# The seams around the feed-forward of a hybrid layer: four output tiles by token halves, plain products placed between the second norm's matmuls, other places and queues where down begins

## The chip, the core and the metric

One core of a Trainium2 chip runs the whole kernel as one program. Its engines run beside each other, each through its own list of instructions: TensorE (PE: matmuls, and loads of their weights), VectorE (DVE), ScalarE (ACT), GpSimd (POOL) and SyncE (SP, which here only issues transfers). An instruction waits until what it reads is there and what it overwrites has been read; all that stands behind it on the same engine waits with it. The metric is the time of one execution on the device in microseconds (us), the median of several runs.

## The reference

One layer, cut to what matters here: the matmuls around the second norm and the shapes. The two mixers ahead of it are not touched.

```python
D_MODEL = 1024; SEQ = 1024; D_FF = 2816; EPS = 1e-6     # BATCH 1, DEPTH 1, all float32

def rms_norm(x, w):
    y = x * lax.rsqrt(jnp.mean(x * x, axis=-1, keepdims=True) + EPS)
    return y * w

def reference(x, norm1_w, w_in, ..., w_out, norm2_w, w_gate, w_up, w_down):
    h = rms_norm(x, norm1_w[l])
    z, xbc, dt_raw, q, k, v = jnp.split(h @ w_in[l], SPLITS, axis=-1)
    y_ssd = ssd_mixer(z, xbc, dt_raw, ...)          # causal convolution, chunked state scan, gated norm
    y_att = diff_attention(q, k, v, ...)            # 8 heads, difference of two softmax maps, head norm
    x = x + jnp.concatenate([y_ssd, y_att], axis=-1) @ w_out[l]         # (1024, 2048) @ (2048, 1024)
    h = rms_norm(x, norm2_w[l])
    return x + (jax.nn.silu(h @ w_gate[l]) * (h @ w_up[l])) @ w_down[l] # 2816 wide in between
```

## The kernel before

Channels lie on the 128 partitions and the 1024 tokens along the free axis, so the model's width is 8 tiles (DK), and a matmul makes 128 channels by 512 tokens, one "token half" (`halves`). float32 products are made of three matmuls: each operand is split into a high part (a cast by ScalarE, line 152) and a low part (operand minus high part, line 153, by VectorE or GpSimd), and `mm3` (lines 163 to 166) adds high x high, high x low and low x high. A piece of weights is loaded by SP into a `wr` buffer, of which there are two, and split (`load_op`).

The **out projection** has eight output tiles. `add_out(d, q...)` puts one quarter of the inner width for tile d on a list of jobs, and `half()` works jobs off. Tiles 0 to 5 take both token halves with one load of each weight piece; tiles 6 and 7 are done for the first half of the tokens, then for the second, with their weights loaded once for each half: 6 x 4 + 2 x 4 x 2 = 40 pieces of 256 KB. After each tile `out_post` (line 1031) adds the residual into `x2[d]`, stores it to `x2d` in DRAM (SP), and sums its squares into `accm`. When a token half is complete, a job `norm2(hf)` follows (line 1045): four matmuls that sum `accm` over the channels (`ps_r2`, line 1050), mean and power -1/2, a transpose (`ps_tr`, line 117), its spreading over a row (line 123), a matmul that broadcasts that row to all partitions (`ps_bc`, line 135), its copy into `accm` by ScalarE (line 136), eight scalings of `x2[d]` by VectorE (line 1059), and eight splits into the operands `a11`, `a12` (first half of the tokens) or `a21`, `a22` (second half).

The **feed-forward** has 22 tiles of 128 inner channels. Two of them are done by plain products (`plain`, line 1108): 24 matmuls, three for each of the 8 tiles of channels, for one tile, for gate or up (u = 0 or 1) and one token half. The first three, (f, u, hf) = (0, 0, 0), (0, 1, 0) and (1, 0, 0), need only the first half's operands; the rest needs the second's. In between GpSimd makes sums and differences of the operands (`sums`, lines 1077 to 1083) for the other 20 tiles, which follow Strassen's scheme with seven products over 2 x 2 blocks instead of eight. The first of these products is `ps_a`.

Gate times up gives `m`. `store_pair` (line 1087) stores for each pair of tiles seven operands of down's seven products into `md` in DRAM: three stores of `m`, and four of sums that GpSimd makes (`ss`, `sd`, lines 1096 to 1104). **Down** takes the 11 pairs in four chunks (3, 3, 3, 2 pairs) and the 8 output tiles in four pairs: a *unit* is a chunk and a pair of output tiles, 7 products of 9 matmuls (6 in the last chunk). `fetch_m` (line 1259) brings the stored operands back into `mr` buffers (four, issued by GpSimd) and splits them into `mo`; `Down.load` brings a unit's weights (`wr`, `in_wdn_dram`, 768 KB, issued by SP); GpSimd makes differences of them (`t`, line 1151) and `make` (line 1288) casts and subtracts. In the first chunk `fetch_m` for all seven products stands ahead of the units; for the other chunks it stands behind each product of the chunk's last unit (`Ahead`). The sums go to `acc` tiles that are loaded from `x2d` (line 1325, eight of 512 KB, GpSimd). Down's tiles lie where those of gate/up lay, since the pools of the latter are closed first; a write there waits for the last reader of what lay there.

The order of instructions on each engine is not the order of the code: a list scheduler with modelled durations picks, when the program is built, the next ready instruction of each engine. What the code fixes is what depends on what, the pools, and the queue on which a transfer is issued.

## Time and profile before

| | |
|---|---|
| median of 3 runs | 1706.17 us (1706.12 to 1708.75) |
| the profiled execution | 1707.36 us |
| its span, first to last instruction | 1705.6 us, 23840 instructions |
| PE busy | 1630.9 us, 96 %, 8237 matmuls |
| VectorE, GpSimd, ScalarE busy | 68 %, 46 %, 46 % |
| DRAM read and written | 107.99 MB, 34.87 MB |

The profile is of one execution. Its span and the 1.8 us around it make the execution's time. "Busy" counts time in which the engine has an instruction under way; a timeline lists an engine's instructions by start, with the idle time before each in brackets and what ended it. SPq in place of SP is that engine's issuing of transfers.

### The profile page before, as it was taken

The page shows a single profiled execution, that of the slowest core. Times are in us where ns is not written, and L with a number is a line of the kernel's source. Part 1 is how long each engine was busy: PE and PEld are TensorE (multiplying, and loading weights), DVE is VectorE, ACT ScalarE, POOL GpSimd, SP SyncE. Part 2 cuts the span into 40 slices and gives each one's busy share as a digit, 9 for nine tenths or more (in the row PEclk, how much of TensorE's full clock was granted, in tenths as well). Part 3 has the DMA queues.
Part 4 walks back from the last instruction along what each step waited for, and adds up shares of the span by engine and source line. Part 5 has one row for each costly group of instructions (what it writes and reads, how often), then busy time and mean ns, then how long its engine had stood idle before and what let it go on. Part 6 is the DMA issues. An engine that isn't in the chain of part 4 may idle for free.

```text
span 1705.6 us, 23840 instructions
## 1 busy us (share of the span) xinstructions
PE 1630.9 (96%) x8237; PEld 1383.0 (81%) x8237; DVE 1155.7 (68%) x2213; ACT 782.3 (46%) x1751; POOL 786.4 (46%) x988
## 2 busy tenths in 40 slices
PE   7899999999999999999999987999999999499998
PEld 7799999999988787877778866888888888388886
DVE  7788788878887567886641249855555554498876
ACT  5576676666565544546321234332333222354531
POOL 5755665665522323333242219644344441565535
PEclk9899999999999999999999988999999999699999
DMA  5100110110011110132152312322332221655533
GB/s 185 38 26 26 50 44 15 43 50 14 14 62 44 50 38 27 49 142 81 62 179 74 106 43 68 136 99 99 105 102 102 99 93 44 253 183 162 162 104 111
DMA packets 72312, 144.40 MB, mean 85 GB/s; under 512 B 8362, under 2 KB 16810, under 8 KB 72192
## 3 DMA queue, kind: packets, MB, share of 16 engines
q1 hardware_dynamic: 53984, 108.93, 18.8%
q0 software_dynamic: 8704, 29.24, 5.2%
q10 hardware_dynamic: 9504, 4.72, 1.0%
q8 instruction: 65, 1.06, 0.3%
q14 instruction: 55, 0.45, 0.1%
HBM read 107.99 MB, written 34.87 MB: 84 GB/s over the span
## 4 chain that ended last, share of the span: by engine, by line
PE 86%; DVE 6%; issue 3%; ACT 2%; DMA 1%; POOL 1%; DVEq 0%; ACTq 0%; POOLq 0%
PE ps_pj L203 5%; PE ps_pj L205 5%; PE ps_pj L204 5%; PE ps_x L481 5%; PE ps_x L482 4%; PE ps_x L483 4%; PE p L166 4%; PE p L165 4%; PE p L164 3%; PE ps_c L164 3%; PE ps_a L166 3%; PE ps_c L165 3%; PE ps_d L166 3%; PE ps_c L166 3%; PE ps_d L164 3%; PE ps_d L165 3%
## 5 line engine op out<-in xcount | busy, mean ns | idle before, releaser
L152 ACT CAST op<-wr 128x512 fp32r<-128x512 f32 x148 | 91.2, 618 | 260.4 <-PE p L166 94.9
L153 DVE TENSOR_TENSOR op<-wr,op 128x512 fp32r<-128x512 f32 x104 | 85.6, 825 | 151.5 <-ACT op L152 143.6
L203 PE MATMUL ps_pj<-wh,xwh 128*128 128x384 f32 (+1 forms) x512 | 175.6, 346 | 6.8 <-ACT wh L146 6.0
L205 PE MATMUL ps_pj<-wh,xwl 128*128 128x384 f32 (+1 forms) x512 | 173.7, 341 | 3.5 <-DVE xwl L270 3.5
L204 PE MATMUL ps_pj<-wl,xwh 128*128 128x384 f32 (+1 forms) x512 | 174.0, 340 | 0.0
L1151 POOL TENSOR_TENSOR t<-wr,t 128x512 f32<-128x512 f32 (+2 forms) x72 | 92.5, 1285 | 152.8 <-issue 123.7
L153 POOL TENSOR_TENSOR op<-wr,op 128x512 fp32r<-128x512 f32 x44 | 58.8, 1336 | 224.8 <-ACT op L152 224.8
L481 PE MATMUL ps_x<-xwh,op 128*128 128x512 f32 x320 | 129.8, 406 | 0.9 <-ACT ya L424 0.9
L482 PE MATMUL ps_x<-xwl,op 128*128 128x512 f32 x320 | 126.7, 396 | 0.0
L483 PE MATMUL ps_x<-xwh,op 128*128 128x512 f32 x320 | 126.5, 395 | 0.0
L1151 POOL TENSOR_TENSOR t<-wr 128x512 f32<-128x512 f32 (+2 forms) x72 | 87.9, 1221 | 62.9 <-DVE op L153 32.9
L378 ACT ACTIVATE pt<-ps_s,nm 128x640 f32<-128x640 f32 (+7 forms) x128 | 94.3, 740 | 44.5 <-DVE nm L373 24.3
L203 PEld LDWEIGHTS ps_pj<-wh,xwh 128*128 128x128 f32 x512 | 97.5, 191 | 7.4 <-ACT wh L146 7.1
L166 PE MATMUL p<-y,op 128*128 128x512 f32 x256 | 101.3, 398 | 0.0
L165 PE MATMUL p<-y,op 128*128 128x512 f32 x256 | 101.2, 397 | 0.0
L205 PEld LDWEIGHTS ps_pj<-wh,xwl 128*128 128x128 f32 x512 | 97.4, 190 | 4.2 <-DVE xwl L270 4.2
L152 ACT CAST op<-t 128x512 fp32r<-128x512 f32 x80 | 49.6, 622 | 111.4 <-PE ps_c L166 53.9
L164 PE MATMUL p<-y,op 128*128 128x512 f32 x256 | 99.5, 399 | 0.0
L153 DVE TENSOR_TENSOR op<-t,op 128x512 fp32r<-128x512 f32 x80 | 77.2, 967 | 31.9 <-ACT op L152 30.9
L204 PEld LDWEIGHTS ps_pj<-wl,xwh 128*128 128x128 f32 x512 | 97.7, 191 | 0.4
L373 DVE TENSOR_REDUCE nm<-ps_s 128x1 f32<-128x640 f32 (+7 forms) x128 | 93.7, 745 | 1.4
L318 POOL TENSOR_TENSOR raw<-raw,w_qk 128x192 f32<-128x192 f32 x56 | 41.1, 734 | 79.4 <-ACT raw L317 46.3
(302 smaller groups left out, 4754.6 us busy)
## 6 DMA issues: line engine op xcount, KB each, us to landing
wr<-in_wgu_dram SPq DMA_DIRECT2D x88, 256.0 KB, 2.8
mr<-md POOLq DMA_DIRECT2D x77, 256.0 KB, 3.2
wr<-in_wqkv_dram SPq DMA_DIRECT2D x28, 384.0 KB, 3.0
wr<-in_wxz_dram SPq DMA_DIRECT2D x40, 256.0 KB, 2.8
wr<-in_wout_dram SPq DMA_DIRECT2D x40, 256.0 KB, 2.8
wr<-in_wdn_dram SPq DMA_DIRECT2D x12, 768.0 KB, 5.0
md<-m SPq DMA_DIRECT2D x33, 256.0 KB, 2.0
md<-ss SPq DMA_DIRECT2D x22, 256.0 KB, 2.4
```

Of the source, the lines that this page charges most:

```text
L152: A.copy(out=op[:, 0:n], in_=src)
L153: eng.tensor_tensor(out=op[:, n : 2 * n], in0=src, in1=op[:, 0:n], op=ALU.subtract)
L164: T.matmul(out=ps, lhsT=wh, rhs=a[:, 0:512], start=first, stop=False, skip_group_check=more)
L165: T.matmul(out=ps, lhsT=wh, rhs=a[:, 512:1024], start=False, stop=False, skip_group_check=more)
L166: T.matmul(out=ps, lhsT=wl, rhs=a[:, 0:512], start=False, stop=last, skip_group_check=more)
L203: T.matmul(out=ps[:, :n], lhsT=xwh[k][:, ts], rhs=wh[:, k % 2, :], start=k == first, stop=False)
L204: T.matmul(out=ps[:, :n], lhsT=xwh[k][:, ts], rhs=wl[:, k % 2, :], start=False, stop=False)
L205: T.matmul(out=ps[:, :n], lhsT=xwl[k][:, ts], rhs=wh[:, k % 2, :], start=False, stop=k == last)
L481: T.matmul(out=ps, lhsT=wh[:, ks], rhs=xwh[k][:, fs], start=k == 0, stop=False)
L482: T.matmul(out=ps, lhsT=wh[:, ks], rhs=xwl[k][:, fs], start=False, stop=False)
L483: T.matmul(out=ps, lhsT=wl[:, ks], rhs=xwh[k][:, fs], start=False, stop=k == DK - 1)
L1151: G.tensor_tensor(out=self.t[name], in0=x, in1=y, op=ALU.subtract)
```

## The change

Seven edits, of which the first two concern the first seam, the others the start of down:

1. `NHALF = 4`: output tiles 4 to 7, not 6 and 7, are done by token halves, with 4 x 4 + 4 x 4 x 2 = 48 weight pieces.
2. `row_t` and `row_b` return their matmul. `norm2` keeps its last channel sum, its transpose and its broadcast in the list `order` (numbers 3 to 5 for the second half), and `issue_after` puts matmuls of `plain` behind one of them on PE: the first 12 of (0, 1, 0) behind the second half's channel sums, its last 12 behind the transpose, the first 12 of (1, 0, 0) behind the broadcast.
3. `x2d` and `md` are separate tensors in DRAM for each tile and each pair, instead of one.
4. The fetches of stored operands (`mr`) are issued by SP instead of GpSimd, with six buffers instead of four.
5. `acc` is loaded in pairs of tiles, each called for in the middle of the unit before instead of all at the start.
6. The operands of the products (`a11` to `s4`) lie in other pools (`place_of`), and the inputs of out take the places of other ones (`tags`).
7. In down, two pads and a pool `wde` set where `mr`, `op` and `wr` lie: `wde` holds `mr` and six of ten `op` buffers.

```diff
+NHALF = 4
...
-    x2d = dp.tile([DK, P, S], F32, name="x2d")
-    md = dp.tile([NPR, len(PRODUCTS), P, 512], F32, name="md")
+    x2d = [dp.tile([P, S], F32, name=f"x2d{d}") for d in range(DK)]
+    md = [dp.tile([len(PRODUCTS), P, 512], F32, name=f"md{i}") for i in range(NPR)]
...
-            for d in range(3, DK - 2):
+            for d in range(3, DK - NHALF):
                 for hq in range(4):
                     add_out(d, hq // 2, hq % 2)
             for hf in range(2):
-                for d in range(DK - 2, DK):
+                for d in range(DK - NHALF, DK):
...
+    order = []
...
-            T.matmul(out=ps[:, t : t + 1], lhsT=accm[...], rhs=ones[:, 0:1], start=True, stop=True)
+            last = T.matmul(out=ps[:, t : t + 1], lhsT=accm[...], rhs=ones[:, 0:1], start=True, stop=True)
...
-        row_t(bank, rtok[:, ts])
+        order.append(last)
+        order.append(row_t(bank, rtok[:, ts]))
...
-        row_b(bank, [sx], accm[:, fs])
+        order.append(row_b(bank, [sx], accm[:, fs]))
...
-    def plain(f, u, hf, last):
+    def plain(f, u, hf, last, gates=(None, None)):
...
         for k in range(DK):
             op = plain_w[(f, u)][k // 4]
-            mm3(ps, ...)
+            gate = gates[k // 4]
+            with tc.issue_after(gate.ins) if gate else nullcontext():
+                mm3(ps, ...)
...
-        plain(f, u, hf, last)
+        plain(f, u, hf, last, {(0, 1, 0): (order[3], order[4]), (1, 0, 0): (order[5], None)}.get((f, u, hf), (None, None)))
...
+    ac.tile([P, S], F32, name="pad0")
     wd = pool(ctx, "wd")
+    wde = pool(ctx, "wde")
...
-            mr = wd.tile([P, 512], F32, tag="mr", name="mr", bufs=4)
-            nc.gpsimd.dma_start(out=mr, in_=md[p0 + i, j])
+            mr = wde.tile([P, 512], F32, tag="mr", name="mr", bufs=6)
+            nc.sync.dma_start(out=mr, in_=md[p0 + i][j])
...
+            if self.c == 0 and j == 3 and d1 + 1 < DK:
+                fetch_acc(d1 + 1)
...
+    def fetch_acc(d0):
+        for d in (d0, d0 + 1):
+            nc.gpsimd.dma_start(out=acc[d], in_=x2d[d])
...
     for j in range(7):
         fetch_m(0, j)
-    for d in range(DK):
-        nc.gpsimd.dma_start(out=acc[d], in_=x2d[d])
+    fetch_acc(0)
```

What this does to the order that is built, at three places. First, TensorE at the second half's norm; `p0` is the result of a plain product, `a11` and `a12` the first half's operands, `a21` the second's. Before:

```order
L165 MATMUL p0_10683<-a12_10405,op_10680 128x512
L166 MATMUL p0_10683<-a12_10405,op_10680 128x512
L164 MATMUL p0_10683<-a12_10409,op_10680 128x512
L165 MATMUL p0_10683<-a12_10409,op_10680 128x512
L166 MATMUL p0_10683<-a12_10409,op_10680 128x512
L117 MATMUL ps_tr_10558<-cst_sb_60,wide_67 40x128
L135 MATMUL ps_bc_10564<-sx_10562,ones_r_69 128x512
L164 MATMUL p0_10710<-a21_10568,op_10601 128x512
L164 MATMUL p0_10805<-a21_10568,op_10638 128x512
L164 MATMUL p0_10831<-a21_10568,op_10675 128x512
L165 MATMUL p0_10710<-a21_10568,op_10601 128x512
```

And in the changed kernel:

```order
L170 MATMUL p0_10703<-a12_10314,op_10700 128x512
L168 MATMUL p0_10703<-a12_10318,op_10700 128x512
L169 MATMUL p0_10703<-a12_10318,op_10700 128x512
L170 MATMUL p0_10703<-a12_10318,op_10700 128x512
L138 MATMUL ps_bc_10621<-sx_10619,ones_r_69 128x512
L168 MATMUL p0_10740<-a11_10290,op_10732 128x512
L169 MATMUL p0_10740<-a11_10290,op_10732 128x512
L170 MATMUL p0_10740<-a11_10290,op_10732 128x512
L168 MATMUL p0_10740<-a11_10294,op_10732 128x512
```

Before, no plain product of the first half stands between transpose and broadcast, nor behind the broadcast: 46 stand ahead of the channel sums (`ps_r2`) and 26 between these and the transpose. Now it is 24 ahead of the sums, 12 between sums and transpose, 12 between transpose and broadcast, and 24 behind it.

Second, the transfers that SP issues where down begins; `m`, `ss` and `sd` are the last operands stored, `wr` down's first weights, `mr` the fetched operands. Before:

```order
L1089 DMA md_77<-m_13729 128x512
L1089 DMA md_77<-ss_13862 128x512
L1089 DMA md_77<-m_13840 128x512 x2
L1089 DMA md_77<-ss_13862 128x512
L1089 DMA md_77<-sd_13863 128x512 x2
L1277 DMA wr_14011<-in_wdn_dram 128x3x512
L1277 DMA wr_14042<-in_wdn_dram 128x3x512
L1277 DMA wr_14106<-in_wdn_dram 128x3x512
```

And changed:

```order
L1279 DMA mr_13963<-md0_84 128x512
L1279 DMA mr_13968<-md1_85 128x512
L1279 DMA mr_13973<-md2_86 128x512
L1279 DMA mr_13978<-md0_84 128x512
L1279 DMA mr_13983<-md1_85 128x512
L1279 DMA mr_13988<-md2_86 128x512
L1100 DMA md10_94<-m_13897 128x512 x2
L1294 DMA wr_14070<-in_wdn_dram 128x3x512
L1294 DMA wr_14101<-in_wdn_dram 128x3x512
L1100 DMA md10_94<-ss_13919 128x512
L1100 DMA md10_94<-sd_13920 128x512 x2
```

The first weights of down have moved ahead of the stores of the last sums, and six fetches of stored operands, which were on GpSimd's list, stand ahead of the last stores of `m`.

Third, GpSimd there; `t` are the differences of down's weights. Before:

```order
L1264 DMA mr_13903<-md_77 128x512
L1264 DMA mr_13908<-md_77 128x512
L1264 DMA mr_13913<-md_77 128x512
L1325 DMA acc0_13880<-x2d_76 128x1024
L1325 DMA acc1_13881<-x2d_76 128x1024
L1325 DMA acc2_13882<-x2d_76 128x1024
L1325 DMA acc3_13883<-x2d_76 128x1024
L1325 DMA acc4_13884<-x2d_76 128x1024
L1325 DMA acc5_13885<-x2d_76 128x1024
L1325 DMA acc6_13886<-x2d_76 128x1024
L1325 DMA acc7_13887<-x2d_76 128x1024
L1151 TENSOR_TENSOR t_14016<-wr_14011 128x384
```

And changed:

```order
L1113 TENSOR_TENSOR sd_13920<-m_13897,sd_13920 128x512
L1344 DMA acc0_13937<-x2d0_76 128x1024
L1344 DMA acc1_13938<-x2d1_77 128x1024
L1164 TENSOR_TENSOR t_14075<-wr_14070 128x384
L1344 DMA acc2_13939<-x2d2_78 128x1024
L1344 DMA acc3_13940<-x2d3_79 128x1024
L1344 DMA acc4_13941<-x2d4_80 128x1024
L1344 DMA acc5_13942<-x2d5_81 128x1024
L1344 DMA acc6_13943<-x2d6_82 128x1024
L1344 DMA acc7_13944<-x2d7_83 128x1024
L1164 TENSOR_TENSOR t_14077<-wr_14070,t_14075 128x384
```

The fetches of `mr` are gone from this list. Six of the eight loads of `acc` now stand between the first difference and the second, which is the one that the second product's weights are made of; before, all eight stood ahead of the first and four fetches between the two.

## Rows read from the trace of the kernel before

**Rows 1.** The page: span, and PE's busy tenths in 40 equal slices.

```profile
span 1705.6 us, 23840 instructions
...
PE   7899999999999999999999987999999999499998
```

**Rows 2.** Windows: stretch, length; busy PE, PEld, DVE, ACT, POOL; clock, DMA share, GB/s.

```profile
960.00:980.00 20.00, 20.00 (x92) 16.41 (x91) 4.63 (x8) 4.98 (x8) 6.68 (x6) 1.00 0.34 119
1029.00:1035.00 6.00, 5.98 (x14) 4.73 (x15) 5.38 (x9) 0.01 (x1) 5.91 (x1) 0.50 0.00 0
1420.00:1440.00 20.00, 20.00 (x87) 16.23 (x87) 9.15 (x13) 4.81 (x8) 3.18 (x3) 1.00 0.16 61
1460.00:1480.00 20.00, 6.10 (x11) 3.13 (x11) 5.82 (x6) 5.19 (x11) 13.05 (x21) 0.50 0.97 368
1478.50:1489.00 10.50, 7.48 (x14) 4.36 (x15) 10.50 (x13) 6.22 (x14) 7.33 (x8) 0.50 0.70 243
```

**Rows 3.** Timeline of PE, first seam: start, us, engine, line, out<-in [idle <-releaser].

```profile
993.18 0.39 PE L166 MATMUL p<-y,op 128*128 128x512 f32 x1
...
998.22 0.79 PE L165 MATMUL p<-a,op 128*128 128x512 f32 x1 [3.94 <-DVE a L153]
...
1019.81 0.47 PE L135 MATMUL ps_bc<-sx,ones_r 40*128 40x512 f32 x1 [1.50 <-DVE sx L123]
...
1029.02 0.79 PE L165 MATMUL p<-a,op 128*128 128x512 f32 x1 [4.97 <-DVE a L153]
...
1053.81 0.51 PE L166 MATMUL p<-a,op 128*128 128x512 f32 x1 [1.46 <-POOL op L153]
...
1063.55 0.47 PE L164 MATMUL ps_a<-a,op 128*128 128x512 f32 x1 [1.57 <-DVE m L1122]
```

**Rows 4.** Timeline of VectorE: the eight scalings of either token half.

```profile
990.55 6.41 DVE L1059 SCALAR_TENSOR_TENSOR x<-x,pk_sb,accm 128x512 f32<-128x512 f32 x8 [4.43 <-ACT accm L136]
...
1020.94 7.42 DVE L1059 SCALAR_TENSOR_TENSOR x<-x,pk_sb,accm 128x512 f32<-128x512 f32 x8 [0.55 <-ACT accm L136]
```

**Rows 5.** Timelines of VectorE and of GpSimd behind the second half's scalings.

```profile
1030.08 0.68 DVE L153 TENSOR_TENSOR s<-s,s 128x512 fp32r<-128x512 f32 x1
...
1044.26 1.57 DVE L153 TENSOR_TENSOR s<-s,s 128x512 fp32r<-128x512 f32 x1
...
1029.09 7.68 POOL L1079 TENSOR_TENSOR x<-x,x 128x512 f32<-128x512 f32 x2 [3.94 <-DVE a L153]
...
1052.04 1.72 POOL L153 TENSOR_TENSOR op<-wr,op 128x512 fp32r<-128x512 f32 x1
```

**Rows 6.** Timelines of SP, ScalarE and PE where down begins.

```profile
1461.31 0.95 SPq L1277 DMA_DIRECT2D wr<-in_wdn_dram  x2
...
1468.11 0.51 ACT L1289 CAST op<-wr 128x384 fp32r<-128x384 f32 x1 [12.29 <-DMA wr<-in_wdn_dram]
...
1469.19 0.80 PE L164 MATMUL ps_a<-mo,op 128*128 128x512 f32 x1 [14.82 <-ACT mo L152]
...
1478.53 0.80 PE L164 MATMUL ps_b<-mo,op 128*128 128x512 f32 x1 [4.19 <-ACT op L1289]
```

**Rows 7.** Timelines of SP and of GpSimd there.

```profile
1456.57 0.32 SPq L1089 DMA_DIRECT2D md<-m  x1
...
1459.31 1.26 POOL L1102 TENSOR_TENSOR sd<-m,sd 128x512 f32<-128x512 f32 x1
1460.86 2.20 POOL L1264 DMA_DIRECT2D mr<-md  x4 [0.30 <-POOL sd L1102]
1463.05 2.62 POOL L1325 DMA_DIRECT2D acc<-x2d  x5
```

**Rows 8.** The tile wr on SP from 1455 us on: down's sixteen weights.

```profile
DMA to landing us min/median/max: 3.6/4.6/11.5
```

**Rows 9.** DMA issues from 1455 to 1475 us: KB each, median us to landing.

```profile
acc<-x2d POOLq DMA_DIRECT2D x8, 512.0 KB, 10.9
...
md<-sd SPq DMA_DIRECT2D x2, 256.0 KB, 2.1
```

More of the change, by code (lines that the diff above doesn't have):

```diff
@@ L1 @@
-from contextlib import ExitStack
+from contextlib import ExitStack, nullcontext
 import concourse.bass as bass
@@ L116, in row_t @@
         ps = bank("ps_tr")
-        T.transpose(ps[0:40, 0:P], wide[:, 0:40], ident)
+        ins = T.transpose(ps[0:40, 0:P], wide[:, 0:40], ident)
         V.tensor_copy(out=wrow, in_=ps[0:40, 0:P])
         V.tensor_tensor(out=wrow[32:40], in0=ps[32:40, 0:P], in1=wrow[32:40], op=ALU.subtract)
+        return ins
     def row_a(spread):
@@ L134, in row_b @@
             ps = bank("ps_bc")
-            T.matmul(out=ps, lhsT=ones_r, rhs=spread[i], start=True, stop=True)
+            ins = T.matmul(out=ps, lhsT=ones_r, rhs=spread[i], start=True, stop=True)
             A.copy(out=dst[:, 512 * i : 512 * i + 512], in_=ps)
+        return ins
     def load_w(wp, src, n, lo_eng, size, wp2=None, parts=1):
@@ L913, in split_y, with place_of @@
     def split_y(src, kk, eng):
-        tags = (("a21", "s1"), ("a12", "s3"), ("a22", "s4"), ("a11", "s2"))[kk // 4]
-        return [
-            split((ra if kk < 8 else rb).tile([P, S], F32R, tag=tag, name="y", bufs=4), src[:, 512 * hf : 512 * hf + 512], eng)
-            for hf, tag in enumerate(tags)
-        ]
+        tags = ((1, "s3"), (0, "a22")), ((1, "s4"), (0, "a21")), ((0, "a11"), (1, "s2")), ((1, "s1"), (0, "a12"))
+        res = {}
+        for hf, tag in tags[kk // 4]:
+            res[hf] = split(place_of(tag).tile([P, S], F32R, tag=tag, name="y", bufs=4), src[:, 512 * hf : 512 * hf + 512], eng)
+        return res
+    def place_of(name):
+        return rb if name in ("a11", "s2", "s1", "a12") else ra
     def fetch(dst, i):
@@ L1033, in out_post @@
         V.tensor_tensor(out=x2[d][:, fs], in0=pd.pop((d, hf)), in1=x2[d][:, fs], op=ALU.add)
-        nc.sync.dma_start(out=x2d[d, :, fs], in_=x2[d][:, fs])
+        nc.sync.dma_start(out=x2d[d][:, fs], in_=x2[d][:, fs])
         if d == 0:
@@ L1049, in norm2 @@
         for t in range(4):
-            T.matmul(out=ps[:, t : t + 1], lhsT=accm[:, (4 * hf + t) * P : (4 * hf + t + 1) * P], rhs=ones[:, 0:1], start=True, stop=True)
+            last = T.matmul(out=ps[:, t : t + 1], lhsT=accm[:, (4 * hf + t) * P : (4 * hf + t + 1) * P], rhs=ones[:, 0:1], start=True, stop=True)
         V.tensor_scalar(out=rtok[:, ts], in0=ps[:, 0:4], scalar1=1.0 / 1024.0, scalar2=EPS, op0=ALU.mult, op1=ALU.add)
         G.tensor_tensor(out=rtok[:, ts], in0=rtok[:, ts], in1=mhalf.broadcast_to([P, 4]), op=ALU.pow)
-        row_t(bank, rtok[:, ts])
+        order.append(last)
+        order.append(row_t(bank, rtok[:, ts]))
         sx = mq.tile([P, 512], F32R, tag="gt", name="sx", bufs=2)[0:40]
         row_a([sx])
-        row_b(bank, [sx], accm[:, fs])
+        order.append(row_b(bank, [sx], accm[:, fs]))
         for d in range(DK):
@@ L1060, in norm2 @@
             name = f"a{1 + hf}{1 + d // 4}"
-            op = (rb if name in ("a11", "a22") else ra).tile([P, S], F32R, tag=name, name=name, bufs=4)
+            op = place_of(name).tile([P, S], F32R, tag=name, name=name, bufs=4)
             ops[(name, d % 4)] = split(op, x2[d][:, fs], V)
@@ L1088, in store_pair @@
         m0, m1 = ms.pop(2 * i), ms.pop(2 * i + 1)
-        put = lambda name, t: nc.sync.dma_start(out=md[i, PRODUCTS.index(name)], in_=t)
+        put = lambda name, t: nc.sync.dma_start(out=md[i][PRODUCTS.index(name)], in_=t)
         for name, t, fs in (("a11", m0, halves[0]), ("a12", m1, halves[0]), ("a22", m1, halves[1])):
@@ L1287, in make @@
         def make(self, src):
-            op = wd.tile([P, 2, 3, P], F32R, tag="op", name="op", bufs=10)[:, :, : self.n]
+            n = Down.slot[0] = (Down.slot[0] + 1) % 10
+            op = (wd if n > 5 else wde).tile([P, 2, 3, P], F32R, tag="op", name="op", bufs=4 if n > 5 else 6)[:, :, : self.n]
             A.copy(out=op[:, 0], in_=src)
@@ L1320, in end @@
             pass
+    def fetch_acc(d0):
+        for d in (d0, d0 + 1):
+            nc.gpsimd.dma_start(out=acc[d], in_=x2d[d])
+    wd.tile([P, 3, 4, P], F32, tag="wr", name="wr", bufs=2)
+    wd.tile([P, 3, P], F32, tag="t", name="t", bufs=4)
+    wd.tile([P, 2, 3, P], F32R, tag="op", name="op", bufs=4)
+    wd.tile([P, 544], F32, name="pad1", bufs=1)
     for j in range(7):
         fetch_m(0, j)
-    for d in range(DK):
-        nc.gpsimd.dma_start(out=acc[d], in_=x2d[d])
+    fetch_acc(0)
     class Ahead(Down):
```

5 lines of the change are left out of this document (3 added, 2 removed).

## Prediction

> **What bounds the kernel now.** I read the page's slices first. TensorE (PE) shows a 9 in nearly every slice of 42.6 us, so what the change can win lies in the few that do not: the 8 and the 7 (slices 24 and 25 of 40, 981 to 1066 us), and the 4 (slice 35, from 1450 us) [rows 1]. Then I cut windows around these places. Just before the second, 87 matmuls fill 20.00 us, so one costs 0.23 us; from 1460 to 1480 us only 11 run, in 6.10 us of 20 [rows 2]. The first place is the seam between the out projection and the feed-forward (seam 1), the second the start of down (seam 2). Third, the timeline of PE with the waits in brackets. Seam 1 has 3.94, 1.50 and 4.97 us of waiting for the second norm, and later 1.46 and 1.57 for weights [rows 3]. Seam 2 begins with one wait of 14.82 us, has another of 4.19, and its first matmuls run at 0.50, the lower of the clock's two levels (1.2 of 2.4 GHz) [rows 2, 6]. Last, the other engines' timelines there: who is late, and what it sat behind.
>
> **Seam 1, up to the second half's operands.** Before, the norm of the first token half has two half tiles of out to run beside; it now has four (4 x 48 matmuls, 44 us at 0.23). Its eight scalings began at 990.55, with the last out matmuls [rows 4]; now 44 us of them follow, so the 3.94 us wait goes. The norm of the second half still comes after all out products. I follow it from the start of the last out matmul, 993.18 before [rows 3], as zero. The same 72 plain products of the first half stand behind it in both kernels, but before, the order puts 46 + 26 of them ahead of the transpose, and nothing beside the rest of the norm. After, the order is 24 products, the four sums over channels, 12, transpose, 12, broadcast, 24.
> - 24 products: to 5.8. The sum of squares is ready by then: add 0.69, square 0.63, add 0.69, some 2.6 with hand-overs.
> - sums, 0.8 (their eight passes are between plain matmuls): 6.6; 12 products: 9.4; transpose 0.3, 12 products: 12.5. Meanwhile the row work, some 1.7 us from the sums to the transpose's input and another 1.7 to the broadcast's, fits under 12 products (2.8) each.
> - broadcast at 12.5. Before, broadcast to the first scaling is 1019.81 to 1020.94, 1.13 us, and from there to the matmul that uses the first low part 1020.94 to 1029.02, 8.08 us [rows 3, 4]: 12.5 + 1.1 + 8.1 = 21.7.
> - Before, the same matmul starts at 1029.02 - 993.18 = 35.8. Gain 14.1. In this stretch PE is still idle some 2.5 us, since 24 + 3 products (6.2) cover only part of the 9.2 from the broadcast on.
> Bounds: the eight scalings take 7.42 us with GpSimd working beside them [rows 4]; the first half's took 6.41 without it [rows 4]. At 1.57 each, as a subtraction in lockstep with GpSimd [rows 5], 5 us would be lost, with the 2.5 us of idle gone too, 2.5 won; 9 to 17 for this term, and I take the rows' 14.1.
>
> **Seam 1, from there to the first Strassen product.** PE then needs 34.5 us to the first matmul of gate/up (1029.02 to 1063.55), with 1.46 + 1.57 of waits [rows 3] and 2.8 us lost to the lower clock at its start (14 matmuls in 5.98 us [rows 2], where 0.23 each is 3.2): 5.8 could go. But VectorE and GpSimd are what this stretch rests on. VectorE's subtraction is 0.68 us in a run of its own and 1.57 in turns with GpSimd [rows 5]; GpSimd's is 1.26 alone [rows 7] and 1.72 here; its first two took 7.68 while VectorE's run lasted [rows 5]. GpSimd's twelfth operation there (1052.04 [rows 5]) makes the weights that PE waits for at 1053.81, and in the new order it is the twelfth again. So a PE that comes earlier waits more: I count 1 us (0 to 5.8). The Trainium skill says the same of the cause: "SBUF — State Buffer", section "Who interferes with whom", has VectorE with two SBUF inputs and a GpSimd read take one port pair in turns, the later one blocked until the first is done. By it nearly nothing is won here, without it all of the waits; the lengthened rows agree with it.
> Extra work: eight more weight pieces (4 tiles in halves instead of 2), each 256 KB, one cast and one subtraction. In 960 to 980 us, where half tiles run already, PE is busy 20.00 of 20 with VectorE 4.63 and ScalarE 4.98 [rows 2]; that is the cover, and the cost is nothing. Without it a late piece would cost a cast and a subtraction, some 2 us.
>
> **Seam 2.** Before, the fetches of the stored products (mr) stand on GpSimd's queue behind the last sum, 1459.31 + 1.26, and leave at 1460.86; eight loads of acc follow, and down's first weights leave at 1461.31 [rows 7, 6]. The stored products were one tensor, so that a fetch waited for the last store; now each pair is one. Their first six fetches leave on SP once the last unit's first product has read its operands, near 1438, where the transfers use 0.16 of the engines [rows 2], and are down by 1445. That does not start down yet: its first weights stand on SP behind the last store of m, 1456.57 [rows 7], and leave near 1457 instead of 1461.3. Landing takes 4.6 us in the median of all sixteen (3.6 the shortest [rows 8]; 6.8 for this one before, 1461.31 to 1468.11 [rows 6]): 1461.5. From landing to the first matmul 1.08 us as before (1468.11 to 1469.19): 1462.6, 6.6 earlier.
> New waits: ScalarE's cast of the second fetched tile writes where the last sums lie, and waits for their last store, issued as the last sum ends, 1460.6 [rows 7]; it takes 2.1 us as the two do now [rows 9], up to 6 with acc and the weights beside it, so 1463 to 1467. Behind it on ScalarE stand all other casts of down. I take 1465, which ends the nine matmuls of the first product near 1468.3 with VectorE's subtractions between. The second product needs a difference from GpSimd, which now has six acc issues (five took 2.62 [rows 7]) ahead of it instead of four fetches that wait for buffers: 1461.7 + 1.0 + 3.2 + 1.0, then, once the first product is out, its copy and a cast: 1469.7. Before it was 1478.53 [rows 6]: 8.8 earlier. From there to 1489 PE lost 7.3 us more (14 matmuls in 10.50 us [rows 2], 3.2 at full clock). After, I count 4: nine matmuls at 0.43 for 0.23 is 1.8, and some 2 for casts and subtractions, since VectorE, busy 10.50 of 10.50 from 1478.5 on [rows 2], has two fewer tiles left to split by then. Sum 8.8 + 3.3 = 12.1; bounds 5 (the weights' lead of 4.4 and little more) and 17 (no wait for the store, clock back at once).
> The later fetches move to SP too. After slice 35 PE is at 9 up to the last slice [rows 1], and its order there is the same; GpSimd is freed of 0.55 us for each (four took 2.20 [rows 7]). I count nothing; the price if the cover fails is the last rival.
>
> **Sum.** 14.1 + 1 + 12.1 = 27.2 us off the profiled execution's 1707.36 (its span of 1705.6 and 1.8 around it): 1680.2. It lies 1.2 above the median of the runs, 1706.17, from which the same sum gives 1679.0, my forecast. The likeliest case by itself, with half of each term's bounds, is 1674 to 1685.
>
> **Rivals.**
> - Transfers bind seam 2. From 1460 to 1480 us they use 0.97 of the engines at 368 GB/s [rows 2], 7.4 MB; acc (4 MB) and two weights (1.6) are still in that window, acc landing 10.9 us after issue [rows 9], so the first product could wait for the store and the second round of fetches for acc. Then only the issue lead, 1461.3 to 1457, is won: 4.3 + 15.1, 1686.8; 1685 to 1692. For it: acc takes long there. Against it: 1.6 MB of the window is gone. The Trainium skill ("DMA: Bandwidth & Descriptors", section "Issuing engines are not separate DMA queues") speaks for it: a second issuing engine saves issue time alone, since all transfers run on the same 16 DMA engines. By it the fetches moved to SP win nothing where transfers fill the window.
> - More is won: the plain products after the norm do not wait for GpSimd, and seam 2 starts with no wait for the store. 16 + 3 + 15: 1672, 1666 to 1675. Against it rows 5, for it that VectorE gets its subtractions done before GpSimd is up.
> - The change does not do what it says: the gate's order holds, but the second norm's chain is as long as before, since VectorE does its plain evictions ahead of it; then seam 1 gives the 3.94 and the low clock behind it, 6, and seam 2 nothing: 1700, or, with down later by the same, no change.
> - Slower: SP's queue. The fetches of a chunk stand behind down's weights, which wait for one of two buffers, for at most one unit: 63 matmuls, 14.5 us. At three changes of chunk that is up to 43.5 us, less the 27.2: 1722.5. It decides from 9.1 us per change on. Against it: such a weight waits for a buffer of two units ago, and six fetches stand ahead.
>
> **Chances.** The forecast's case 0.57, transfers bind 0.19, more 0.12, the change not doing it 0.07 (half of them within 0.2%), slower 0.05. A difference of 0.2%, 3.4 us, is what can be told from no change. So faster 0.92, same 0.03, slower 0.05; range 1666 to 1692, which leaves out the last two and the ends of the others.
>
> **What would show it.** Right: no wait of PE between the last out matmul and the broadcast; 21 to 23 us from that matmul to the first product with a second-half low part; waits for weights of up to 4 us after it, and the first Strassen product some 33 us after; six fetches down before 1446 (shifted by seam 1's gain); down's first matmul some 8.6 us after the last of gate/up (14.8 of wait before), then a short wait for the second tile. Wrong: scalings of over 1.2 us each, a first down matmul later than 11 us after gate/up, or waits after 1500 us.

## The result, and the profile after

The changed kernel takes 1683.99 us, the median of 4 runs (1682.36 to 1685.48), against 1707.41 us for the kernel before in 4 runs beside it (1706.12 to 1708.75). The ratio is 0.9863, with an interval of 0.9845 to 0.988: faster by 23.4 us. The forecast was 1679.0, the range 1666 to 1692. The profiled execution took 1682.61 us, 1680.8 of it span, 24.8 less than the span before.

The page's span and PE's slices, which answer to [rows 1]: of the two places below 9, the first is now one slice of 9 and one of 8, and the 4 is a 6.

```profile
span 1680.8 us, 23898 instructions
...
PE   7899999999999999999999998999999999699999
```

To see where the 24.8 us came from I use the prediction's zero, the start of the last out matmul (A), and a second one, the start of the last matmul of gate/up (B: 1453.98 before, 1443.39 after).

| stretch | before | after | won | forecast |
|---|---|---|---|---|
| up to A | 993.18 | 992.54 | 0.6 | 0 |
| A to the first low part of the second half | 35.84 | 22.07 | 13.8 | 14.1 |
| from there to the first Strassen product | 34.53 | 34.51 | 0.0 | 1 |
| from there to B | 390.43 | 394.27 | -3.8 | 0 |
| B to the last matmul | 244.26 | 233.08 | 11.2 | 12.1 |
| last matmul to the end of the span | 7.36 | 4.33 | 3.0 | 0 |

**Seam 1.** PE's timeline, as in [rows 3]. Nothing waits between the last out matmul and the broadcast, which comes 12.79 us after it; the first product with a low part of the second half comes 9.28 later, after one wait of 2.31.

```profile
1005.33 0.50 PE L138 MATMUL ps_bc<-sx,ones_r 40*128 40x512 f32 x1
...
1014.61 0.50 PE L169 MATMUL p<-a,op 128*128 128x512 f32 x1 [2.31 <-DVE a L157]
...
1034.86 0.50 PE L170 MATMUL p<-a,op 128*128 128x512 f32 x1 [1.93 <-DVE op L157]
...
1049.12 0.47 PE L168 MATMUL ps_a<-a,op 128*128 128x512 f32 x1 [1.75 <-DVE m L1135]
...
1052.96 0.50 PE L168 MATMUL ps_b<-s,op 128*128 128x512 f32 x1 [0.81 <-ACT op L156]
1054.56 0.50 PE L170 MATMUL ps_b<-s,op 128*128 128x512 f32 x1 [0.34 <-DVE op L157]
...
1067.06 0.50 PE L168 MATMUL ps_c<-s,op 128*128 128x512 f32 x1 [2.00 <-DVE u L1216]
```

VectorE's scalings and one of its lockstep subtractions, as in [rows 4, 5], take what they took, 7.48 and 1.56 us, and so do GpSimd's first two operations behind them:

```profile
1006.48 7.48 DVE L1070 SCALAR_TENSOR_TENSOR x<-x,pk_sb,accm 128x512 f32<-128x512 f32 x8 [0.29 <-ACT accm L139]
...
1029.87 1.56 DVE L157 TENSOR_TENSOR s<-s,s 128x512 fp32r<-128x512 f32 x1
```

```profile
1014.69 7.69 POOL L1090 TENSOR_TENSOR x<-x,x 128x512 f32<-128x512 f32 x2 [3.94 <-DVE a L157]
```

**Seam 2.** The timeline of PE, then ScalarE, then SP, as in [rows 6, 7]. Down's first matmul is 8.74 us behind B instead of 15.21, and the second product's (ps_b) 18.99 instead of 24.55.

```profile
1452.13 0.80 PE L168 MATMUL ps_a<-mo,op 128*128 128x512 f32 x1 [8.34 <-ACT mo L156]
...
1457.66 0.79 PE L168 MATMUL ps_a<-mo,op 128*128 128x512 f32 x1 [3.26 <-ACT mo L156]
...
1462.38 0.79 PE L168 MATMUL ps_b<-mo,op 128*128 128x512 f32 x1 [1.14 <-ACT op L1307]
```

```profile
1451.04 0.51 ACT L1307 CAST op<-wr 128x384 fp32r<-128x384 f32 x1 [5.80 <-DMA wr<-in_wdn_dram]
...
1456.98 2.70 ACT L156 CAST mo<-mr 128x512 fp32r<-128x512 f32 x5 [4.91 <-DMA md<-sd]
```

```profile
1428.25 2.76 SPq L1279 DMA_DIRECT2D mr<-md  x6
...
1446.40 0.96 SPq L1294 DMA_DIRECT2D wr<-in_wdn_dram  x2
...
1448.67 1.66 SPq L1100 DMA_DIRECT2D md<-sd  x2
```

The fetches leave 15 us ahead of B, and ScalarE waits for the weights, 1446.40 to 1451.04. Its cast of the second tile then waits 4.91 us, named as the store of sd (issued 1450.0). The issues with their landing, as in [rows 9]: the store takes 6.8 us where it took 2.1.

```profile
acc<-x2d POOLq DMA_DIRECT2D x8, 512.0 KB, 9.4
...
md<-sd SPq DMA_DIRECT2D x2, 256.0 KB, 6.8
```

Windows (columns as in [rows 2]) over seam 1's two stretches of low clock, down's start, and the three changes of chunk (near 1522, 1580 and 1638 us): PE does 26 matmuls in the 20 us where it did 11, then 32 in the 10.50 us from ps_b on where it did 14, at a granted 0.84 for 0.50, and is full in the last three.

```profile
1014.60:1020.60 6.00, 5.99 (x19) 4.77 (x20) 5.38 (x9) 0.44 (x1) 5.91 (x1) 0.72 0.00 0
1035.70:1039.10 3.40, 3.40 (x10) 2.62 (x9) 3.40 (x4) 1.96 (x4) 3.40 (x3) 0.50 0.23 80
1449.40:1469.40 20.00, 11.09 (x26) 6.92 (x27) 12.03 (x15) 11.14 (x23) 13.63 (x17) 0.59 1.03 386
1462.40:1472.90 10.50, 9.25 (x32) 7.16 (x33) 10.50 (x15) 7.96 (x17) 5.58 (x5) 0.84 1.00 378
1515.00:1535.00 20.00, 20.00 (x89) 16.42 (x88) 20.00 (x33) 12.09 (x23) 5.61 (x5) 1.00 0.76 250
1570.00:1590.00 20.00, 20.00 (x89) 16.43 (x88) 20.00 (x34) 13.75 (x27) 4.46 (x4) 1.00 0.76 239
1630.00:1650.00 20.00, 20.00 (x89) 16.39 (x88) 17.84 (x32) 6.96 (x16) 9.57 (x10) 1.00 0.34 114
```

**The end.** The last store lands 3.2 to 3.3 us behind the last matmul's start in both kernels, at 1701.45 and 1679.73. Before, GpSimd's closing DRAIN, by which the program ends, was still under way then: it takes 11.91 us from GpSimd's last sums on, 1692.88 to 1704.79. After, it takes 5.62 and is over at 1673.61. The rows give it for the kernel before, the changed one, and the experiment mr_gpsimd, which has the fetches on GpSimd's queue (least, median and greatest duration in ns of the three DRAINs of that line; the greatest is the one meant):

```profile
L1423 POOLq DRAIN  x3: 51/93/11912, 1692.9 to 1705.3; - x3
...
L1451 POOLq DRAIN  x3: 46/102/5622, 1668.0 to 1680.6; - x3
...
L1451 POOLq DRAIN  x3: 46/93/11921, 1672.4 to 1684.8; - x3
```

### The profile page after: what moved, and what is told of

The parts are those of the page before. It is cut to its first block, busy times and chain, and to the rows that moved or that the text cites. A ratio compares the mean times of both kernels' runs of the same rounds, so it can differ in the third digit from the quotient of the medians.

```text
span 1680.8 us, 23898 instructions
## 1 busy us (share of the span) xinstructions
PE 1623.5 (97%) x8237; PEld 1378.7 (82%) x8237; DVE 1162.8 (69%) x2217; ACT 786.1 (47%) x1759; POOL 754.4 (45%) x915
## 4 chain that ended last, share of the span: by engine, by line
PE 85%; DVE 6%; ACT 3%; issue 3%; POOL 2%; DMA 1%; SPq 0%; DVEq 0%; ACTq 0%; POOLq 0%
PE ps_pj L207 5%; PE ps_pj L209 5%; PE ps_pj L208 5%; PE ps_x L485 5%; PE ps_x L486 4%; PE ps_x L487 4%; PE p L170 3%; PE p L168 3%; PE p L169 3%; PE ps_c L170 3%; PE ps_c L169 3%; PE ps_d L168 3%; PE ps_c L168 3%; PE ps_d L169 3%; PE ps_d L170 3%; PE ps_a L170 3%
## 5 line engine op out<-in xcount | busy, mean ns | idle before, releaser
L156 ACT CAST op<-wr 128x512 fp32r<-128x512 f32 x156 | 96.2, 618 | 258.2 <-PE ps_d L170 77.9
L157 DVE TENSOR_TENSOR op<-wr,op 128x512 fp32r<-128x512 f32 x108 | 89.6, 831 | 145.7 <-ACT op L156 142.9
L157 POOL TENSOR_TENSOR op<-wr,op 128x512 fp32r<-128x512 f32 x48 | 64.4, 1343 | 211.3 <-ACT op L156 211.3
L410 PE MATMUL po<-v,wt 128*128 128x128 f32 x576 | 77.5, 276 | 0.0
```

The lines of the kernel that those rows point to most:

```text
L156: A.copy(out=op[:, 0:n], in_=src)
L157: eng.tensor_tensor(out=op[:, n : 2 * n], in0=src, in1=op[:, 0:n], op=ALU.subtract)
```

## The experiments

Each is the changed kernel with the edit shown; "..." stands for lines left out. Positions are of its profiled execution, counted from its own A or B.

**Seam 1 alone** (seam1_only): down as before.

```diff
-            mr = wde.tile([P, 512], F32, tag="mr", name="mr", bufs=6)
-            nc.sync.dma_start(out=mr, in_=md[p0 + i][j])
+            mr = wd.tile([P, 512], F32, tag="mr", name="mr", bufs=4)
+            nc.gpsimd.dma_start(out=mr, in_=md[p0 + i, j])
...
-            op = (wd if n > 5 else wde).tile([P, 2, 3, P], F32R, tag="op", name="op", bufs=4 if n > 5 else 6)[:, :, : self.n]
+            op = wd.tile([P, 2, 3, P], F32R, tag="op", name="op", bufs=10)[:, :, : self.n]
```

> Down is fetched, placed and queued as before; only the first seam's edits stay. Theory: the two seams are independent. From the last out matmul to the first matmul with a second-half low part 22.1 us (after: 22.07, before: 35.84); the first unit of gate/up then waits some 3.8 us for weights as in the changed kernel; from the last matmul of gate/up to down's first 15.2 us and to its second product 24.6 as before. Time 1707.4 - 10.6 = 1696.8. Rival: the 3.8 us come from the new places of down's tiles; then 1693.

1700.0 us, 0.9955 (0.994 to 0.997). The first low part comes at A + 22.03, B to the end takes 251.04 (251.62 before, 237.41 after), so each seam's stretch goes with its own edits. Down's first product comes at B + 12.95, not at the 15.2 expected, the second at 24.02. The first seam's edits alone give 7.8 us, and the others 16 on top of them. The time is 3.2 us above the expectation: from the first Strassen product to B it takes 397.82 us, not 394.27. About 2 us of that lie in the first unit, most of them where the granted clock was 0.52 behind the wait of ps_c (9 matmuls in the 3.00 us from 1069 on; it was 1.00 there in the changed kernel), and 1.5 are a slower pace of PE over all of gate/up, for which see the last section.

**No gates** (no_gates) and **two half tiles** (half2): the parts of seam 1.

```diff
-        plain(f, u, hf, last, {(0, 1, 0): (order[3], order[4]), (1, 0, 0): (order[5], None)}.get((f, u, hf), (None, None)))
+        plain(f, u, hf, last, (None, None))
```

> Four output tiles by halves, but no gates: in the order that is built 29 plain matmuls stand ahead of the channel sums, 26 ahead of the transpose, 17 ahead of the broadcast and none behind it. Theory: broadcast at about 19 us behind the last out matmul (12.8 with gates), first low part of the second half at 28 us (22.1), PE idle 9 us between. In this order the first unit's weights are issued ahead of the store of ss, so if that store holds them up in the changed kernel, 3.8 us come back: 1684 + 6.2 - 3.8 = 1686. Rival: it is GpSimd's sums that hold the first unit up, then 1690.

```diff
-NHALF = 4
+NHALF = 2
```

> Gates kept, but only two output tiles by token halves. Theory: the first half's norm has less to run beside, so PE waits some 4 us for it and runs 2 us slower behind that wait (the clock); from the last out matmul to the first low part of the second half about 28 us instead of 22.1: 1684 + 6 = 1690. Rival: the four half tiles are not needed once plain matmuls are gated, 1684.

1688.09 us (0.9869 to 0.9903) and 1692.54 (0.9896 to 0.9925). Without gates the broadcast comes at A + 18.05 and the low part at 27.35; with two half tiles at 18.71 and 28.0; with both parts at 12.79 and 22.07, before at 26.63 and 35.84. Each part alone gives 7.8 to 8.5 of the 13.8 us, and the other then adds 5.3 to 5.9. What goes missing is read off PE: without gates the second norm's wait is back, with two tiles the first norm's [rows 3]. half2's time is 8.5 us above the changed kernel's, more than these 5.9, since its first unit and its pace are slow as in seam1_only (first Strassen product to B 397.44).

```profile
1021.80 0.80 PE L169 MATMUL p<-a,op 128*128 128x512 f32 x1 [4.99 <-DVE a L157]
```

```profile
997.45 0.50 PE L169 MATMUL p<-a,op 128*128 128x512 f32 x1 [4.39 <-DVE a L157]
```

**Fetches on GpSimd's queue** (mr_gpsimd), **one tensor for the stored products** (md_one), **the fetched tiles in a place that comes free late** (mr_late_place): which part of down's new start matters.

```diff
-            nc.sync.dma_start(out=mr, in_=md[p0 + i][j])
+            nc.gpsimd.dma_start(out=mr, in_=md[p0 + i][j])
```

> The fetches of stored operands go back to GpSimd's queue, with six buffers and all else as changed. In the order built the first six still leave ahead of the last sums. Theory: what brings the first fetches forward is that the stored products are separate tensors with places that are free early, so down's first matmul still comes 8.7 us behind gate/up; but the second round of fetches waits for buffers on GpSimd ahead of later differences of weights, which costs 2 to 5 us by the fourth product: 1687. Rival: the queue is what matters, first matmul at 15 us, 1695.

```diff
-    md = [dp.tile([len(PRODUCTS), P, 512], F32, name=f"md{i}") for i in range(NPR)]
+    md = dp.tile([NPR, len(PRODUCTS), P, 512], F32, name="md")
```

> The stored products (md) are one tensor in DRAM again; all else as changed. The prediction's account: a fetch then waits for the last store of any pair, the first six fetches stand on SP until behind the last sums, and down's first matmul comes some 15 us behind gate/up instead of 8.74: 1691. Rival, from the order as built, in which no fetch names a store as what it waits for: stores and fetches are told apart within one tensor, the split does nothing, 1684.

```diff
-            mr = wde.tile([P, 512], F32, tag="mr", name="mr", bufs=6)
+            mr = wd.tile([P, 512], F32, tag="mr", name="mr", bufs=6)
...
-            op = (wd if n > 5 else wde).tile([P, 2, 3, P], F32R, tag="op", name="op", bufs=4 if n > 5 else 6)[:, :, : self.n]
+            op = wde.tile([P, 2, 3, P], F32R, tag="op", name="op", bufs=10)[:, :, : self.n]
```

> The six mr buffers change places with four op buffers: they lie where gate/up's last weights and temporaries lay, and the order as built puts the first fetches behind the last m stores and down's first weights behind the last sd store. Separate tensors and SP's queue stay. Theory: it is the place, free since the last unit's first product, that let the fetches leave early; now down's first matmul comes 14 to 16 us behind gate/up's last (8.74 in the changed kernel, 15.21 before): 1690. Rival: the queue or the separate tensors did it, 8.7 us still: 1684.

mr_gpsimd 1686.17 us (0.9857 to 0.9886), md_one 1685.86 (0.9851 to 0.9883): neither stands apart from the changed kernel, and B to the end is 239.21 and 237.82 (237.41). On GpSimd the six fetches leave at 1430.17, 15.7 us ahead of its B (15.1 on SP). mr_late_place: 1688.97 us (0.9876 to 0.9906), down's first matmul at B + 21.06, later than before the change, and 244.4 to the end. Its fetches leave at 1446.32 and its weights at 1450.83, 4.4 us later than after the change, since the order changed with the place:

```profile
1446.32 0.86 SPq L1279 DMA_DIRECT2D mr<-md  x2
...
1450.83 1.50 SPq L1294 DMA_DIRECT2D wr<-in_wdn_dram  x2
```

```profile
1463.80 0.51 ACT L1307 CAST op<-wr 128x384 fp32r<-128x384 f32 x1 [2.69 <-DMA wr<-in_wdn_dram]
...
1464.36 0.79 PE L168 MATMUL ps_a<-mo,op 128*128 128x512 f32 x1 [20.67 <-ACT op L1307]
```

So the place is what lets the fetches leave early; for the queue and the split of the tensor these runs show no more than 2.2 and 1.9 us, within the scatter. But the fetches are not what this kernel's first product waits for: the first had landed at 1449.20. It waits for the weights, as in the changed kernel, and these are 12.97 us under way (1450.83 to 1463.80) where they were 4.64, with all six fetches, acc and the stores beside them. Of the 12.3 us by which this product is later, 4.4 are their later place in the order and some 8 their landing. So what the early fetches win here is, as far as these rows show, that the weights do not land beside them; no run holds the weights' order fixed with late fetches.

**The first unit's weights ahead of the first stores** (store0_late): the loss of 3.8 us behind the first Strassen product.

```diff
-    store_pair(0)
...
+        if isinstance(steps[0], GateUp):
+            store_pair(0)
```

> The stores of the first pair's operands come in the code behind the preparation of the first unit, so that in the order built the unit's last two weight pieces leave SP ahead of the store of ss, which waits for GpSimd. Theory: the waits of 0.81 and 0.34 us before the first unit's second product go, VectorE gets its splits done earlier, and the 2.00 us wait of ps_c goes for the most part: first Strassen matmul to last of gate/up 391 us instead of 394: 1681. Rival: GpSimd and VectorE in turns are the limit there, and only 1 us comes back: 1683.

From the first Strassen product to B it takes 391.54 us instead of 394.27, and ps_b's waits are gone; ps_c's wait is 1.05 instead of 2.00. no_gates, whose order also has these weights ahead of the store, takes 391.56; four kernels with the changed kernel's order there (md_one, mr_late_place, mo_shift, acc_late) take 394.37 to 394.62. The time, 1682.59 (0.9834 to 0.9869), shows no difference of its own; in the profiled execution A came 2.3 us later. The cause is in SP's and GpSimd's rows of the changed kernel:

```profile
1034.83 5.34 SPq L1195 DMA_DIRECT2D wr<-in_wgu_dram  x3
1046.17 0.33 SPq L1100 DMA_DIRECT2D md<-ss  x1
1046.59 1.34 SPq L1195 DMA_DIRECT2D wr<-in_wgu_dram  x3
```

```profile
1044.40 1.74 POOL L1107 TENSOR_TENSOR ss<-m 128x512 f32<-128x512 f32 x1
...
1050.97 1.29 POOL L1164 TENSOR_TENSOR t<-wr,t 128x512 f32<-128x512 f32 x1 [3.15 <-DMA wr<-in_wgu_dram]
```

The store of ss waits for GpSimd's sum, 1044.40 + 1.74; behind it on SP stand weight pieces whose buffers were free, and GpSimd and ScalarE then wait for these. In the kernel before, SP issued all seven weights ahead of the store:

```profile
1049.25 11.66 SPq L1182 DMA_DIRECT2D wr<-in_wgu_dram  x7
...
1063.43 0.33 SPq L1089 DMA_DIRECT2D md<-m  x1
1063.80 0.43 SPq L1089 DMA_DIRECT2D md<-ss  x1
```

**The sums of the second half on VectorE** (sums_dve): whether GpSimd holds the stretch behind the broadcast.

```diff
-        G.tensor_tensor(out=t, in0=a, in1=c, op=ALU.subtract)
+        V.tensor_tensor(out=t, in0=a, in1=c, op=ALU.subtract)
...
-        G.tensor_tensor(out=b, in0=b, in1=a, op=ALU.subtract)
+        V.tensor_tensor(out=b, in0=b, in1=a, op=ALU.subtract)
```

> The sixteen sums of operands ahead of the Strassen units are made by VectorE instead of GpSimd. Theory: in the changed kernel both engines slow each other (1.57 us a subtraction on VectorE, 1.72 a sum on GpSimd, against 0.68 and 1.26 alone); 32 operations of 0.68 on VectorE take 22 us where the two engines in turns took 37, so the scalings take 6.4 instead of 7.5 us, the waits of 1.93 and 1.75 us go, and from the last out matmul to the first Strassen one it is 52 us instead of 56.6: 1680. Rival: VectorE with sixteen operations more becomes the bound, and PE waits for weights behind them: 1688.

1679.52 us (0.9814 to 0.9845). The scalings take 5.39 us instead of 7.48, a subtraction behind them 0.68, and the first Strassen product comes at A + 52.99 instead of 56.58, though VectorE has sixteen more operations. SP's order changes with it: six of the first unit's weight pieces now leave ahead of the first store, from 1035.99 on, so the 392.79 us from there to B, for 394.27, are not the sums' alone.

```profile
1005.36 5.39 DVE L1070 SCALAR_TENSOR_TENSOR x<-x,pk_sb,accm 128x512 f32<-128x512 f32 x8 [0.29 <-ACT accm L139]
...
1023.92 0.68 DVE L157 TENSOR_TENSOR s<-s,s 128x512 fp32r<-128x512 f32 x1
```

**The first fetched tiles in places off the last sums** (mo_shift) and **acc's later loads behind later differences** (acc_late): what holds the second product.

```diff
-            mo[(c, j, i)] = split(rd.tile([P, S], F32R, tag="op", name="mo", bufs=24), mr, V)
+            n19 = len(mo) % 24 < 19
+            mo[(c, j, i)] = split(rd.tile([P, S], F32R, tag="op" if n19 else "op5", name="mo", bufs=19 if n19 else 5), mr, V)
```

> The fetched operands lie so that none of the first ones falls on the last sums (sd, ss). Theory: ScalarE's cast of the second tile then doesn't wait for the last sd store (4.91 us in the changed kernel), the first product has no 3.26 us gap, and the second product starts some 4 us earlier, near 14.7 us behind gate/up's last matmul instead of 18.99. Transfers fill the next 25 us, so part is given back: 1681. Rival: transfers or GpSimd's differences bind, and the second product starts at 18 to 19 us all the same: 1684.

```diff
-                G.tensor_tensor(out=self.t[name], in0=x, in1=y, op=ALU.subtract)
+                order[0:1] = [G.tensor_tensor(out=self.t[name], in0=x, in1=y, op=ALU.subtract)]
...
+        with tc.issue_after(order[0].ins) if d0 else nullcontext():
```

> acc tiles 2 to 7 are loaded only behind later differences on GpSimd's queue. Theory: GpSimd makes the second difference 3.2 us earlier, and the last sd store lands sooner than in 6.8 us, since 3 MB less compete with it; the cast of the second tile starts some 3 us earlier and so does the second product (16 us behind gate/up instead of 18.99): 1681. Rival: the store takes as long with the weights beside it, or acc then comes late for the second unit: 1684 or more.

ps_b comes at B + 15.19 in mo_shift and at 16.25 in acc_late (18.99), and B to the end takes 234.13 and 233.61 us (237.41). The times, 1682.61 (0.9837 to 0.9873) and 1682.36 (0.9833 to 0.9867), overlap the changed kernel's, so the profiles show 3 to 4 us that the runs' times can't confirm. In acc_late the first product starts later (B + 11.62) and the second is still earlier: its start does not set the rest.

**Everything early** (best2) and **what had gained, together** (best3).

```diff
-    store_pair(0)
...
+            cast[len(mo)] = cast[0]
...
-            wr = wd.tile([P, 3, 4, P], F32, tag="wr", name="wr", bufs=2)[:, : self.n]
+            wr = wde.tile([P, 3, 4, P], F32, tag="wr", name="wr", bufs=2)[:, : self.n]
...
+            with tc.issue_after(cast[3 * n].ins) if self.c == 0 and self.d == 0 and 0 < n < 6 else nullcontext():
```

Beside these lines best2 has the edits of sums_dve, store0_late and acc_late, and one like mo_shift's with 18 + 5 tiles.

> All that helped put together, and down's first weights, their differences and two op buffers also at places that are free early, with the first casts of weights queued behind the operands that their product needs (23 mo buffers instead of 24). Theory: seam 1 as with the sums on VectorE (53 us from the last out matmul to the first Strassen one), no wait of that unit for weights (391.5 us to the last of gate/up), down's first matmul some 4 us behind it, the second product at 9 us and the third at 14 us instead of 18.99 and 23.2; transfers fill these 25 us, so down gains 8: 1670. Rival: transfers bind and acc comes late, down gains 4: 1675.

The theory fell. Down's first product starts at B + 2.82 and ps_b at 9.28, but B to the end takes 240.12, more than after the change, and the time is 1682.34 (0.983 to 0.9872). The early casts bring VectorE's splits in a row of six, 9.35 us in turns with GpSimd. On GpSimd three differences of the early weights, 1.45 us each, now stand between the last sums, which take 1.52 to 1.72 us instead of 1.26, so the last sum starts at B + 10.05 and not at 5.33. The last store waits for it, and the second round of fetches stands behind the store on SP and leaves at B + 12.20 (9.76 after the change):

```profile
1441.23 9.35 DVE L159 TENSOR_TENSOR mo<-mr,mo 128x512 fp32r<-128x512 f32 x6
...
1448.33 1.71 POOL L1115 TENSOR_TENSOR sd<-m,sd 128x512 f32<-128x512 f32 x1
```

```profile
1445.58 4.81 SPq L1102 DMA_DIRECT2D md<-sd  x2
1450.48 19.32 SPq L1283 DMA_DIRECT2D mr<-md  x15
```

```diff
+            n19 = len(mo) % 24 < 19
...
+        with tc.issue_after(order[0].ins) if d0 else nullcontext():
...
+            with tc.issue_after(cast[3 * n].ins) if self.c == 0 and self.d == 0 and n in (1, 2) else nullcontext():
```

best3 has the edits of mo_shift, acc_late, sums_dve and store0_late, and holds two casts of weights back behind those of the operands.

> The single steps that helped, without the earlier weights of the kernel best2: sums of operands on VectorE, the first unit's weights ahead of the store of ss, fetched operands off the last sums, acc tiles 2 to 7 late, and the first product's casts of operands ahead of the second product's weights on ScalarE. Theory: the gains add up where they lie in different places. Seam 1 as in best2 (52 us from the last out matmul to the first Strassen one); down's first matmul 9 us behind gate/up's last, its second product 14 us, and from gate/up's last to the end 232.5 us instead of 237.4: 1673.5. Rival: VectorE's splits and the transfers are the limit of down's first 25 us in every order, so mo_shift and acc_late win the same 3 us, not 6: 1676.

1677.74 us in 5 runs, 0.9818 (0.9804 to 0.9831): below both kernels, its interval clear of the changed one's but not of sums_dve's. The gains do not add. From A to B it takes 445.05 us, with the sums alone (sums_dve) 445.78, with the weights alone (store0_late) 448.35, after the change 450.85: 5.1 and 2.5 us come to 5.8 together. In sums_dve's order six of the weights are ahead of the stores already. Down's come to even less than one of them, 236.52 from B to the end. There PE waits 3.48 us for a weight's low part; VectorE makes it in 0.54, but behind two others that took 3.46 in turns with GpSimd:

```profile
1459.75 0.80 PE L172 MATMUL ps_a<-mo,op 128*128 128x512 f32 x1 [3.48 <-DVE op L1315]
```

```profile
1455.30 3.46 DVE L1315 TENSOR_TENSOR op<-wr,op 128x384 fp32r<-128x384 f32 x2
...
1459.15 0.54 DVE L1315 TENSOR_TENSOR op<-wr,op 128x384 fp32r<-128x384 f32 x1
```

## Why the prediction was right, and where it was not

- **Seam 1 up to the second half's operands: right.** 12.79 us to the broadcast where 12.5 was worked out, 22.07 to the low part for 21.7, 13.8 won for 14.1. no_gates and half2 show that both parts are needed. The eight more weight pieces cost nothing: A came no later.
- **"So a PE that comes earlier waits more": right in the time, not in the wait.** The stretch took 34.51 us for 34.53, with the same 117 matmuls. But PE's waits in it came to 3.68 us for 3.77: VectorE's scalings began 14.5 us earlier too, so the whole row of engines moved with PE. The 1.2 us that its start won at the clock (19 matmuls in 5.99 us for 14 in 5.98) were lost again behind the wait of 1.93, where the granted clock was 0.50 once more (10 matmuls in 3.40 us). That wait is now for a low part that VectorE makes, not for GpSimd's twelfth operation. That VectorE and GpSimd in turns hold the stretch back is shown by sums_dve: with the sixteen sums taken from GpSimd, the first Strassen product comes 3.6 us earlier, 2.7 of them in this stretch. The Trainium skill's rule ("SBUF — State Buffer", section "Who interferes with whom": a VectorE operation with two SBUF inputs and a GpSimd read lock one another out of one shared port pair) agrees with it: 7.48 against 5.39 us for the same eight scalings, 1.56 against 0.68 for a subtraction.
- **The sum's step "from there to the first Strassen product" ended too early.** I counted nothing behind that product; the first unit there lost 3.8 us. A store that waits for GpSimd stands ahead of free weights on SP, and store0_late takes back 2.7 of it. About 1 us stays open. I had read SP's order where down begins and not here.
- **"The stored products were one tensor, so that a fetch waited for the last store": wrong.** With one tensor the fetches leave as early and down starts at B + 9.31. What let them go is the place of their tiles, by mr_late_place. That they do not start down by themselves was right: there too its first product waits for the weights, which land late beside late fetches.
- **Down's first product: right**, B + 8.74 for 8.6, on the weights' lead as worked out.
- **The wait for the store: right in place, mis-sized.** The store was taken to land in 2.1 to 6 us; beside acc and the weights it took 6.8 (2.1 before, [rows 9]), so ScalarE's cast came 2.6 us later than the 1465 of the prediction (1454.4 once the 10.6 us by which B moved are taken off), and ps_b at B + 18.99 where 15.7 was expected. Taking the place away (mo_shift) brings it to 15.19. Behind it more came back than I counted, 5.6 us for 3.3: the granted clock in the 10.50 us from ps_b on was 0.84, not 0.50. So the term, 12.1, measured 11.2 by two errors of opposite sign.
- **"The later fetches move to SP too ... I count nothing": right for down's pace, wrong at the end.** From the last matmul to the end of the span it took 7.36 us before and 4.33 after. GpSimd's closing DRAIN takes 11.91 to 11.93 us in the three kernels whose fetches GpSimd issues (before, seam1_only, mr_gpsimd) and 5.6 in the eleven whose fetches SP issues, where it is over before the last store lands. mr_gpsimd differs from the changed kernel by the queue alone, so the queue sets this length. How much of it shows depends on when GpSimd's last sums come: in mr_gpsimd they come 2.4 us earlier before the last matmul than in the kernel before, and its end takes 4.97 us. What DRAIN waits for, no run shows.
- **The rivals.** "Transfers bind seam 2" is right for the store alone; the issue lead and the first product went as forecast. That the queue is worth little where down begins fits the Trainium skill ("DMA: Bandwidth & Descriptors", section "Issuing engines are not separate DMA queues": another issuing engine saves issue time only): mr_gpsimd's 2.2 us lie within the scatter. "SP's queue" at the changes of chunk is refuted: with 0.23 us for each matmul, PE had lost 19.9 us 30 us behind B and 20.4 at 60, and is full at all three changes.

Of the 24.8 us, the terms of the sum gave 25.0, where 27.2 were forecast; the first unit's loss and the shorter end, neither foreseen, nearly cancel. The time came out right partly for that reason, which is luck.

## What to carry to other kernels

Work put beside a chain wins only up to the next place where TensorE waits for its feeders: work out the next stretch too, up to where TensorE's pace is its own again. On an issuing queue look for a store that waits for a slow engine: the loads behind it wait with it, however free their buffers are. A transfer that is to leave early needs a place that comes free early; which queue issued it mattered little here until the end, where GpSimd's closing DRAIN was 6.3 us longer with the fetches on its queue. Starting a stage earlier is given back where its producers then collide with the work that the stage before still needs (best2). Gains that were each measured alone may be one gain (best3).

## What the runs showed that was not expected

GpSimd's subtraction of 1.26 us took 6.14 when it fell into a run of VectorE's in sums_dve; VectorE's own subtractions kept their 0.68 us each. GpSimd's two operations beside VectorE's run of splits, 7.69 us together (7.68 in [rows 5]), were a smaller case of it. In the changed kernel, in lockstep, both were slowed (1.56 on VectorE).

```profile
1029.83 6.14 POOL L157 TENSOR_TENSOR op<-wr,op 128x512 fp32r<-128x512 f32 x1 [30.06 <-ACT op L156]
```

PE's own pace differs a little between executions at the same granted clock: over the 300 us from 1110 to 1410, in the middle of gate/up, the changed kernel does 1293 matmuls and seam1_only 1288, 0.4% fewer, with no wait in either. The same happened in half2 and mr_gpsimd; before and the others do 1293 or so. It is worth 1.5 us in gate/up and bounds what single profiles can tell apart; I did not find its cause.

```profile
1110.00:1410.00 300.00, 300.00 (x1293) 243.19 (x1292) 160.49 (x216) 91.71 (x154) 127.03 (x93) 1.00 0.28 98
```

```profile
1110.00:1410.00 300.00, 300.00 (x1288) 241.30 (x1287) 158.91 (x216) 91.46 (x155) 124.27 (x90) 1.00 0.28 97
```
